# Value pages of a paged attention asked for two at a time behind pieces of the projections, and summed in twelve segments

## The chip, the core and the metric

The kernel runs on one core of a Trainium2 chip. Its time is the device time of one execution in microseconds (us). Before the change three runs took 2256.08, 2256.88 and 2257.73 us, a median of 2256.88. A profiled execution gives the order of the instructions on each engine: TensorE (PE for its matrix products, PEld for the loading of its stationary operand), VectorE (DVE), ScalarE (ACT), GpSimd (POOL), and SyncE (SP), whose queue asks for most transfers from HBM.

## The reference

The program is one step of a decoder layer for 256 prompt tokens and 8 sequences of 4 new tokens each, 288 columns in all, in float32:

```python
h = h + 1/2 * SwiGLU(RMSNorm(h))                     # half-step FFN 1
h = h + W_out[ norm(conv group) | norm(FoX group) ]  # token mixing
h = h + 1/2 * SwiGLU(RMSNorm(h))                     # half-step FFN 2
h = h + sigmoid(W_g RMSNorm(h)) * (W_p p[layer])     # per-layer input
```

The mixing projects the normed state to a short gated convolution (1024 columns each of B, C and h), to queries, keys and values of 8 heads of 128, and to forget gates. The prompt attends to itself. Each sample sequence attends to its new tokens and to 1024 past rows, which lie in 8 pages of 128 rows, picked by a page table:

```python
v_past = cache_v[page_table].reshape(DB, P, N_HEADS, HEAD_DIM)
...
p = jax.nn.softmax(s, axis=-1)
return jnp.einsum('bhqk,bkhd->bqhd', p.astype(v_all.dtype), v_all)
```

So 8 sequences of 8 pages, 64 value pages of 128 rows by 1024 floats (512 KB each), are multiplied by the probabilities and summed. The change is about how these 64 pages come in and when they are summed.

## The kernel before

**Products.** Every projection is computed with weights as the stationary operand and the 288 columns as the moving one. A weight piece is 512 KB: four blocks of 128 input features by 256 output features. SP loads it into a slot `raw0` to `raw6` (line 256), ACT and DVE split it into a high and a low part (line 294), and TensorE makes three products for each block and each half of the outputs (lines 340 and 342), 24 in all. The function `pair` makes the pieces for 256 outputs; one of its pieces is called a piece here. Splits run five half pieces ahead of the products.

**Order.** The program builds a list of steps. A step is a function, with the weights or pages that it needs. `run_steps` goes through the list, calls `load_upto` for as many items ahead as `state["ahead"]` says, and then the function. A planner afterwards orders the instructions of each engine by readiness, on its own estimate of times, and sets the semaphores; so the order of steps is a priority rather than a fixed order, except where a dependency is added by hand.

**The attention.** In the mixing the key, convolution, value and first half of the output projection form a list of 96 pieces, `fill`. Work of the attention is put between them with `at(i, ...)`, ahead of piece i. Key pages are read in eight pairs of sequences (line 761, up to piece 47). At 48 `v_start` opens the space for values. At 50 and 52 `probs_t` turns the probabilities, at 69 to 86 come the prompt heads.

**The values before.** `v_round` (line 818) sums one page of each of four sequences: round r of group gi takes page r of sequences 4 gi to 4 gi + 3. There are 16 rounds, at 51 and then every 2.7 pieces (round 12 at 82). A page has 1024 columns, two banks of 512. For each bank four products (line 828) with a stationary operand of 32 columns stand side by side in TensorE's four groups of 32 columns, one for each sequence, so a round is two fours. The trace records two instructions for each such product, 16 for a round. After the eighth round of a group `sample_out` adds the new tokens' values (line 841) and gathers the heads out of the two banks.

**The pages' way in.** A round's four pages are items in the same list as the weights. `load_upto` takes them in turn, and POOL asks for each with an indirect transfer (line 261). A page has one of seven slots: `raw4` to `raw6`, which the weights give up meanwhile (they rotate over four slots from the first page on), three of its own (`v0` to `v2`), and the place of the second group's scores, once these are turned. A request waits until the products of the slot's former page are done. POOL also does elementwise work of the convolution, of the residual and of the prompt's masks, all in one queue with the requests. `state["ahead"]` is 12 items, pages and weights together, from `v_start` on.

Of the kernel before, what the change touches and what calls it, by code (L numbers as in the profile page):

```python
# [16 lines left out]
F32 = mybir.dt.float32  # L17
# [8 lines left out]
P = 128  # L26
# [4 lines left out]
DT = 4  # L31
NS = DB * DT
# [4 lines left out]
PAGES = 8  # L37
# [6 lines left out]
RAW = 7  # L44
HALVES = 5
# [6 lines left out]
KPAIRS = (1, 8, 14, 21, 27, 34, 40, 47)  # L52
WEIGHTS = 4
VPAGES = 3
AHEAD = 12
WARM = (NT, NT, NT)
VSTEP = 2.7

GAINS = ("norm_mix", "norm_ffn2", "norm_ple", "norm_final", "norm_conv_out", "norm_attn_out", "conv_w")
A_ROWS = dict(norm_mix=D, norm_ffn2=D, norm_ple=D, norm_final=D, norm_conv_out=CB * P, norm_attn_out=NH * P,  # L60
# [36 lines left out]
def build(nc, tc, ctx, A, O):  # L97
# [3 lines left out]
    v, s, g, pe, sy = nc.vector, nc.scalar, nc.gpsimd, nc.tensor, nc.sync  # L101
# [43 lines left out]
    at = 0  # L145
# [92 lines left out]

    steps = []
    items = []  # L240
    state = dict(wslot=0, pages=0, through=False, ahead=RAW, loaded=0, split=0, used=0, halves_used=0, chunk=0, lead=HALVES)

    def load_upto(n, parts=None):
        while state["loaded"] < min(n, len(items)):
            it = items[state["loaded"]]
            if it["kind"] == "p" and "vx" not in W:
                return
            if it["kind"] == "w":
                state["wslot"] = (state["wslot"] + 1) % (WEIGHTS if state["pages"] and not state["through"] else RAW)
                t = rawp.tile([P, it["nk"], 256], F32, name="wraw", tag=f"raw{state['wslot']}")  # L250
                src = it["src"]
                if parts is not None:
                    cuts = (0, 1, 2, 3, 4) if state["loaded"] < 2 else (0, 2, 4)
                    parts.append([(t[:, a:b], src[:, a:b]) for a, b in zip(cuts, cuts[1:])])
                else:
                    d = sy.dma_start(t, src)
                    if state["used"] < 24:
                        tc.keep_in_program_order(d)
            else:
                t = page_tile()  # L260
                g.indirect_dma_start(out=t, out_offset=None, in_=it["src"],  # L261
                                     in_offset=bass.IndirectOffsetOnAxis(ap=it["rows"], axis=0))
            it["tile"] = t
            state["loaded"] += 1

    def page_tile():

# [42 lines left out]
    def page(src, j):  # L310
        return dict(kind="p", src=src, rows=idx[:, j:j + 1])

    def pair(src, c0, kts, act, evac, k_of=lambda k: k, late=0, tag="mm", rows_first=False):

        st = {}
        out = []
        chunks = [kts[i:i + 4] for i in range(0, len(kts), 4)]
        for ci, ks in enumerate(chunks):
            it = weight(src, ks[0], len(ks), c0)

            def fn(ci=ci, ks=ks, it=it, only=None):
                if ci == 0 and not only:
                    st["ps"] = [bank(tag, BANKS[tag]) for _ in range(2)]
                last = ci == len(chunks) - 1
                if only is None:
                    split_upto(state["halves_used"] + state["lead"])
                if not only:
                    state["chunk"] += 1
                for b in range(2):
                    o = st["ps"][b][:, :NT]  # L330
                    for j, k in enumerate(ks):
                        if only not in (None, j):
                            continue
                        hi, lo = it["parts"][j // 2 * 2]
                        w = slice(b * P, b * P + P)
                        xh, xl = act(k_of(k))
                        f = ci == 0 and j == 0
                        l = last and j == len(ks) - 1
                        for x in (xh, xl) if rows_first else (xl, xh):
                            pe.matmul(o, hi[:, j % 2, w], x, start=f, stop=False)  # L340
                            f = False
                        state["product"] = pe.matmul(o, lo[:, j % 2, w], xh, start=False, stop=l)  # L342
                    if only not in (None, len(ks) - 1):
                        continue
                    if b == 0:
                        run_deferred()
                    if last and late:
                        defer(lambda b=b, o=o: evac(b, o), late)
                    elif last:
                        evac(b, o)  # L350
                state["halves_used"] += len(ks) // 2 if only is None else only % 2

            if rows_first:
                out.extend(([] if j else [it], lambda j=j, fn=fn: fn(only=j)) for j in range(len(ks)))
                continue
            out.append(([it], fn))
        return out

# [457 lines left out]
                              t[:NS, :P].rearrange("s (c b x) -> s b c x", c=4, b=4)[:, b])  # L816
        M["PT", gi] = pt

    def v_round(gi, r):
        its = [page(A["cache_v"], (4 * gi + b) * PAGES + r) for b in range(4)]  # L820

        def fn():
            if r == 0:
                M["va", gi] = [bank("va", BANKS["va"]) for _ in range(2)]
                M["pv", gi] = M["PT", gi].rearrange("s (r b x) -> s r b x", b=4, x=32)
            for e in range(2):
                for b in range(4):
                    pe.matmul(M["va", gi][e][32 * b:32 * b + 32, :], M["pv", gi][:, r, b],  # L828
                              its[b]["tile"][:, e * 512:e * 512 + 512], start=r == 0, stop=False, tile_position=(0, 32 * b))
            if r == PAGES - 1:  # L830
                if gi == 1:
                    state.update(through=True, wslot=WEIGHTS - 1)
                sample_out(gi)
        return (its, fn)

    def sample_out(gi):
        mx = W["vv"][0]
        for b in range(4):
            for e in range(2):
                rows = slice(NS * e, NS * e + NS)  # L840
                pe.matmul(M["va", gi][e][32 * b:32 * b + 32, :], M["pv", gi][rows, 8, b], M["vs"][rows], start=False, stop=True,
                          tile_position=(NS * e, 32 * b))
        o = mx.tile([P, P], F32, name="so", tag="so", bufs=2)
        for hh in range(NH):
            src = M["va", gi][hh // 4][:, hh % 4 * P:hh % 4 * P + P]
            m = const("headmask")[:, hh:hh + 1]
            if hh == 0:
                v.tensor_scalar(o, src, m, None, ALU.mult)
            else:
                v.scalar_tensor_tensor(o, src, m, o, ALU.mult, ALU.add)  # L850
        defer(lambda: sample_turn(gi, o), 4 if gi == 0 else 2)

    def sample_turn(gi, o):
        mx = W["vv"][0]
        t = ktbank()
        pe.transpose(t[:, :P], o, ident)
        for half in range(2):
            v.tensor_copy(M["oS"][:, 4 * half:4 * half + 4, 16 * gi:16 * gi + 16].rearrange("p c (b t) -> p c b t", t=DT),
                          t[:, :P].rearrange("p (b c a t) -> p a c b t", c=4, a=2, t=DT)[:, half])
        if gi == 1:  # L860
            s.dma_start(O["v_prompt"].rearrange("(j p) c -> p j c", p=P), M["vn"])
            for e in range(2):
                s.dma_start(O["v_sample"][:, 512 * e:512 * e + 512], M["vs"][NS * e:NS * e + NS])
            for hh in range(NH):
                split(za[hh][0][:, SEQ:], za[hh][1][:, SEQ:], M["oS"][:, hh, :], gain("norm_attn_out", hh))
            sq = mx.tile([P, NH, NS], F32, name="sqS")
            s.activation(sq, M["oS"], AF.Square)
            v.tensor_reduce(acc[:, SEQ:], sq.rearrange("p h n -> p n h"), AX.X, ALU.add)
# [137 lines left out]
    def v_start():  # L1006
        for n in ("kq", "kt"):
            closed(n)
        opened("vv", "right")
        opened("vp", "right")  # L1010
        opened("vx", "right")
        state["ahead"] = AHEAD
        vv = W["vv"][0]
        M["vn"] = vv.tile([P, 2, NH * P], F32, name="vn")
        M["vs"] = vv.tile([2 * NS, NH * P // 2], F32, name="vs")
        M["oS"] = vv.tile([P, NH, NS], F32, name="oS")
# [25 lines left out]
    def at(i, *fns):  # L1042
        marks.setdefault(i, []).extend(fns)
# [37 lines left out]
    at(KPAIRS[3], lambda: new_scores(0), lambda: new_scores(1))  # L1081
    at(27, lambda: softmax(0))
    at(49, lambda: softmax(1))
    at(48, v_start)
    at(50, lambda: probs_t(0))
    at(52, lambda: probs_t(1))
    for r in range(2 * PAGES):
        at({12: 82}.get(r, int(51 + VSTEP * r)), v_round(r // PAGES, r % PAGES))
    for hh in range(NH):
        at(int(69 + 2.5 * hh), lambda hh=hh: prompt_head(hh))  # L1090
    at(80, lambda: norm_scale(rsc, acc2, CB * P, 2))
# [163 lines left out]
```

## Time and profile before

| What | us |
|---|---|
| Median of three runs | 2256.88 |
| The profiled execution | 2257.42 |
| Its span, first to last instruction | 2255.6 |
| TensorE busy with products | 2239.8 |
| Value products (line 828), 256 instructions, busy | 31.8 |
| Page requests on POOL (line 261), 64, busy | 64.6 |

Busy time of a group is the union of its instructions. Products are pipelined: each has a duration of some 290 ns while the next starts about 129 ns after it, so start-to-start distances tell what an instruction costs, not durations. A row of the order of time gives start, length, engine, line, operation, tiles, shape and count of instructions merged, and in brackets the engine's idle time before it with what ended it. A row of waits gives who waited for whom, the total in us, the number of times and the longest. A row on a stretch of time gives its length, each engine's busy time, TensorE's granted clock, the share of time in which the 16 transfer engines were busy, and GB/s.

### The profile page before, as it was taken

To read this page: it belongs to the slowest core of one execution; us is meant where nothing else is said; L and a number is where in the kernel's file an instruction comes from. 1 tells how busy PE (TensorE), PEld (TensorE's weight loads), DVE (VectorE), ACT (ScalarE), POOL (GpSimd) and SP (SyncE) were. 2 spreads that over 40 slices of the span, in tenths; PEclk is the share of its full clock that TensorE was granted. 3 is DMA by queue.
4 is the path that set the end of the run, shared out by engine and by line. 5 is a ranking of instruction groups with operands and counts; after the bars stand their busy time and mean duration, and the time that the engine had idled before them with its cause. 6 is when DMAs were issued, how large, how long until landed. Compare 5 with 4: busy or idle time off the path is not lost.

```text
span 2255.6 us, 44318 instructions
## 1 busy us (share of the span) xinstructions
PE 2239.8 (99%) x17387; PEld 2183.4 (97%) x17387; DVE 1343.2 (60%) x2413; ACT 1046.8 (46%) x1859; POOL 324.3 (14%) x399
## 2 busy tenths in 40 slices
PE   9999999999999999999999999999999999999997
PEld 9999999999999999888888999999999999999997
DVE  7555555555555686456566875555555555555865
ACT  6444444444444553344344554444444444444654
POOL 1020000000000113344446210000000000000211
PEclk9999999999999999999999999999999999999999
DMA  7575555555555546888988455545555555555552
GB/s 265 172 248 170 170 175 169 169 172 174 169 169 170 169 171 239 330 309 296 330 322 297 170 172 162 180 160 183 172 169 169 175 170 170 169 171 175 168 173 101
DMA packets 342850, 443.37 MB, mean 197 GB/s; under 512 B 17409, under 2 KB 307089, under 8 KB 342641
## 3 DMA queue, kind: packets, MB, share of 16 engines
q1 hardware_dynamic: 320928, 366.25, 49.3%
q0 software_dynamic: 20480, 71.67, 8.9%
q8 instruction: 136, 2.23, 0.4%
q10 hardware_dynamic: 1232, 2.62, 0.3%
q14 instruction: 74, 0.60, 0.1%
HBM read 435.41 MB, written 5.07 MB: 195 GB/s over the span
## 4 chain that ended last, share of the span: by engine, by line
PE 99%; DMA 1%; DVE 0%; issue 0%; ACT 0%; SPq 0%; DVEq 0%; ACTq 0%
PE mm L340 61%; PE mm L342 31%; PE va L340 1%; PE va L828 1%; PE va L761 1%; PE va L342 1%; DMA page<-in_cache_v_dram,idx 0%; PE kt L340 0%; DVE h L1181 0%; DMA h<-in_x_dram 0%; PE kt L342 0%; PE kt L882 0%; PE kt L915 0%; PE kt L906 0%; PE kt L881 0%
## 5 line engine op out<-in xcount | busy, mean ns | idle before, releaser
L340 PE MATMUL mm<-x,whi 128*128 128x288 f32 x7360 | 1430.5, 291 | 0.0
L294 DVE TENSOR_TENSOR wlo<-wraw,whi 128x512 fp32r<-128x512 f32 (+1 forms) x1388 | 975.9, 707 | 739.6 <-ACT whi L294 701.5
L294 ACT ACTIVATE whi<-wraw 128x512 fp32r<-128x512 f32 (+1 forms) x1388 | 861.8, 628 | 869.9 <-PE mm L340 782.6
L340 PEld LDWEIGHTS mm<-x,whi 128*128 128x128 f32 x7360 | 1163.4, 187 | 15.9 <-issue 13.5
L342 PE MATMUL mm<-x,wlo 128*128 128x288 f32 x3680 | 1067.4, 290 | 0.1
L342 PEld LDWEIGHTS mm<-x,wlo 128*128 128x128 f32 x3680 | 690.7, 188 | 0.3 <-DVE wlo L294 0.3
L340 PE MATMUL mm<-hid,whi 128*128 128x288 f32 x2816 | 544.8, 290 | 0.0
L340 PEld LDWEIGHTS mm<-hid,whi 128*128 128x128 f32 x2816 | 445.2, 187 | 0.0
L342 PE MATMUL mm<-hid,wlo 128*128 128x288 f32 x1408 | 408.3, 290 | 0.0
L412 POOL TENSOR_TENSOR sr<-sg,rs 128x288 f32<-128x288 f32 x88 | 71.6, 814 | 1383.7 <-ACT sg L410 1383.7
L342 PEld LDWEIGHTS mm<-hid,wlo 128*128 128x128 f32 x1408 | 264.3, 188 | 0.0
L432 DVE SCALAR_TENSOR_TENSOR h<-mm,h 128x288 f32<-128x288 f32 x192 | 85.6, 455 | 19.4 <-PE mm L342 19.4
L738 POOL DMA_INDIRECT KT<-in_cache_k_dram,idx x64 | 65.9, 1030 | 129.4 <-DVE idx L168 52.2
L410 ACT ACTIVATE sg<-tg 128x288 f32<-128x288 f32 x88 | 39.0, 444 | 97.9 <-DVE tg L408 97.8
L419 ACT ACTIVATE hid<-hd 128x288 fp32r<-128x288 f32 x88 | 39.2, 445 | 93.4 <-DVE hd L417 93.3
L234 POOL TENSOR_TENSOR acc<-acc,sq 128x288 f32<-128x288 f32 x52 | 44.0, 846 | 219.7 <-ACT sq L233 217.2
L261 POOL DMA_INDIRECT page<-in_cache_v_dram,idx x64 | 64.6, 1010 | 67.4 <-PE va L828 44.8
L420 DVE TENSOR_TENSOR hid<-hd,hid 128x288 fp32r<-128x288 f32 x88 | 40.2, 457 | 22.0 <-ACT hid L419 22.0
L340 PE MATMUL mm<-zc,whi 128*128 128x288 f32 x256 | 52.0, 297 | 0.0
L340 PE MATMUL va<-x,whi 128*128 128x288 f32 x256 | 51.1, 293 | 0.8 <-ACT whi L294 0.8
L417 DVE TENSOR_TENSOR hd<-mm,sr 128x288 f32<-128x288 f32 x86 | 39.1, 455 | 16.7 <-PE mm L342 16.7
L408 DVE TENSOR_TENSOR tg<-mm,rs 128x288 f32<-128x288 f32 x84 | 37.9, 452 | 14.1 <-PE mm L342 13.1
(237 smaller groups left out, 1061.0 us busy)
## 6 DMA issues: line engine op xcount, KB each, us to landing
wraw<-in_w_ffn_up_dram SPq DMA_DIRECT2D x173, 512.0 KB, 3.4
wraw<-in_w_ffn_gate_dram SPq DMA_DIRECT2D x172, 512.0 KB, 3.4
wraw<-in_w_ffn_down_dram SPq DMA_DIRECT2D x160, 512.0 KB, 3.2
wraw<-in_w_in_dram SPq DMA_DIRECT2D x96, 512.0 KB, 5.1
wraw<-in_w_out_dram SPq DMA_DIRECT2D x32, 512.0 KB, 4.5
wraw<-in_w_ple_gate_dram SPq DMA_DIRECT2D x32, 512.0 KB, 3.5
wraw<-in_w_ffn_down_dram SPq DMA_DIRECT2D x32, 256.0 KB, 2.7
wraw<-in_w_ple_proj_dram SPq DMA_DIRECT2D x8, 256.0 KB, 2.7
```

The lines of the kernel that those rows point to most:

```text
L234: (v if k >= KT - last_on_v else g).tensor_tensor(acc, acc, sq, ALU.add)
L261: g.indirect_dma_start(out=t, out_offset=None, in_=it["src"], in_offset=bass.IndirectOffsetOnAxis(ap=it["rows"], axis=0))
L294: for i in s.activation(hi, x, AF.Copy), v.tensor_tensor(lo, x, hi.bitcast(F32), ALU.subtract):
L340: pe.matmul(o, hi[:, j % 2, w], x, start=f, stop=False)
L342: state["product"] = pe.matmul(o, lo[:, j % 2, w], xh, start=False, stop=l)
L410: s.activation(u, t, AF.Silu)
L412: g.tensor_tensor(r, u, rs, ALU.mult)
L417: v.tensor_tensor(t, o, sg[b], ALU.mult)
L419: s.activation(H["hi"][:, k, :], t, AF.Copy)
L420: v.tensor_tensor(H["lo"][:, k, :], t, H["hi"][:, k, :].bitcast(F32), ALU.subtract)
L432: v.scalar_tensor_tensor(h[:, k, :], o, 0.5, h[:, k, :], ALU.mult, ALU.add)
L738: d = g.indirect_dma_start(out=t[:, i].rearrange("p h s -> p (h s)"), out_offset=None, in_=A["cache_k"], in_offset=bass.IndirectOffsetOnAx ...
```

## The change

- Pages leave the list of weights. `v_round` returns no items; its pages go to a list `wanted`. `load_upto` handles weights alone.
- A new `ask_pages` asks for pages in order, two at most, in each piece's function, after its splits and ahead of its products. The request is given a dependency on the last product made so far, that is, of the piece before. It asks only while fewer than six pages (seven from page 12 on) are asked and not yet taken up by a segment. At the head of a segment it is called once more for any page of the segment that is still missing, without that dependency.
- `v_round` takes any run of consecutive pages. `VENDS` cuts the 32 pages of each group into segments: 4, 4, 6, 6, 6, 6 in the first group and 6, 6, 6, 6, 4, 4 in the second. They are put at pieces 51, 53, 57, 61, 65, 69, 73, 78, 82, 86, 88 and 91.
- In the second bank the sequences are turned by two column groups, so that pages five and six of a segment fill four groups with their two halves. `sample_out` and `sample_turn` follow; the latter makes three copies in place of two for each group.
- The weights go over to four slots at piece 44 by an explicit switch, with 4 items ahead, and 6 items ahead (weights alone) from `v_start`, in place of 12 for both. Back to seven slots after the last segment, as before.

```diff
-AHEAD = 12
+VENDS = ((4, 8, 14, 20, 26, 32), (6, 12, 18, 24, 28, 32))
...
+    def ask_pages(count, upto=None):
+        while count and "vx" in W and state["pages"] < len(wanted):
+            n = state["pages"]
+            if n >= (state["eaten"] + (6 if n < 12 else 7) if upto is None else upto):
+                return
+            it = wanted[n]
+            it["tile"] = t = page_tile()
+            d = g.indirect_dma_start(out=t, out_offset=None, in_=it["src"],
+                                     in_offset=bass.IndirectOffsetOnAxis(ap=it["rows"], axis=0))
+            if upto is None:
+                tc.add_manual_dep(d.ins, state["product"].ins.name, mybir.DependencyInfo(
+                    mybir.DependencyClass.Sync, mybir.DependencyReason.DATA), reason="pace")
+            count -= 1
...
                 if only is None:
                     split_upto(state["halves_used"] + state["lead"])
+                    ask_pages(2)
...
-    def v_round(gi, r):
-        its = [page(A["cache_v"], (4 * gi + b) * PAGES + r) for b in range(4)]
+    def v_round(gi, pages):
+        its = [page(A["cache_v"], (4 * gi + n % 4) * PAGES + n // 4) for n in pages]
+        wanted.extend(its)
 
         def fn():
-            if r == 0:
+            ask_pages(len(wanted), state["eaten"] + len(pages))
+            state["eaten"] += len(pages)
+            if pages[0] == 0:
...
-            for e in range(2):
-                for b in range(4):
-                    pe.matmul(M["va", gi][e][32 * b:32 * b + 32, :], M["pv", gi][:, r, b],
-                              its[b]["tile"][:, e * 512:e * 512 + 512], start=r == 0, stop=False, tile_position=(0, 32 * b))
+            whole = [(i, e) for e in range(2) for i in (range(4) if e == 0 else (2, 3, 0, 1))]
+            for i, e in whole + [(i, e) for e in range(2) for i in range(4, len(pages))]:
+                r, b = divmod(pages[i], 4)
+                c = 32 * ((b + 2 * e) % 4)
+                pe.matmul(M["va", gi][e][c:c + 32, :], M["pv", gi][:, r, b], its[i]["tile"][:, e * 512:e * 512 + 512],
+                          start=r == 0, stop=False, tile_position=(0, c))
...
-        for half in range(2):
-            v.tensor_copy(M["oS"][:, 4 * half:4 * half + 4, 16 * gi:16 * gi + 16].rearrange("p c (b t) -> p c b t", t=DT),
-                          t[:, :P].rearrange("p (b c a t) -> p a c b t", c=4, a=2, t=DT)[:, half])
+        for half, to, at, n in (0, 0, 0, 4), (1, 0, 2, 2), (1, 2, 0, 2):
+            v.tensor_copy(M["oS"][:, 4 * half:4 * half + 4, 16 * gi:16 * gi + 16].rearrange("p c (b t) -> p c b t", t=DT)[:, :, to:to + n],
+                          t[:, :P].rearrange("p (b c a t) -> p a c b t", c=4, a=2, t=DT)[:, half][:, :, at:at + n])
...
-        state["ahead"] = AHEAD
+        state["ahead"] = WEIGHTS + 2
...
+    at(44, lambda: state.update(narrow=True, ahead=WEIGHTS))
...
-    for r in range(2 * PAGES):
-        at({12: 82}.get(r, int(51 + VSTEP * r)), v_round(r // PAGES, r % PAGES))
+    for gi, ends in enumerate(VENDS):
+        for a, b in zip((0,) + ends, ends):
+            at(int(51 + VSTEP * ((32 * gi + b) / 4 - 1)), v_round(gi, range(a, b)))
```

More of the change, by code (lines that the diff above doesn't have):

```diff
@@ L240, in build @@
     items = []
-    state = dict(wslot=0, pages=0, through=False, ahead=RAW, loaded=0, split=0, used=0, halves_used=0, chunk=0, lead=HALVES)
+    state = dict(wslot=0, pages=0, narrow=False, ahead=RAW, loaded=0, split=0, used=0, halves_used=0, chunk=0, lead=HALVES, eaten=0)
     def load_upto(n, parts=None):
@@ L245, in load_upto @@
             it = items[state["loaded"]]
[L246 to L258, printed above, removed]
-            else:
-                t = page_tile()
-                g.indirect_dma_start(out=t, out_offset=None, in_=it["src"],
-                                     in_offset=bass.IndirectOffsetOnAxis(ap=it["rows"], axis=0))
+            state["wslot"] = (state["wslot"] + 1) % (WEIGHTS if state["narrow"] else RAW)
@@ L263, in load_upto @@
+            t = rawp.tile([P, it["nk"], 256], F32, name="wraw", tag=f"raw{state['wslot']}")
+            src = it["src"]
+            if parts is not None:
+                cuts = (0, 1, 2, 3, 4) if state["loaded"] < 2 else (0, 2, 4)
+                parts.append([(t[:, a:b], src[:, a:b]) for a, b in zip(cuts, cuts[1:])])
+            else:
+                d = sy.dma_start(t, src)
+                if state["used"] < 24:
+                    tc.keep_in_program_order(d)
             it["tile"] = t
@@ L264, in load_upto @@
             state["loaded"] += 1
+    wanted = []
+    def ask_pages(count, upto=None):
[11 more added lines that the diff above has]
+            count -= 1
@@ L817, in probs_t @@
         M["PT", gi] = pt
-    def v_round(gi, r):
-        its = [page(A["cache_v"], (4 * gi + b) * PAGES + r) for b in range(4)]
+    def v_round(gi, pages):
+        its = [page(A["cache_v"], (4 * gi + n % 4) * PAGES + n // 4) for n in pages]
+        wanted.extend(its)
         def fn():
-            if r == 0:
+            ask_pages(len(wanted), state["eaten"] + len(pages))
+            state["eaten"] += len(pages)
+            if pages[0] == 0:
                 M["va", gi] = [bank("va", BANKS["va"]) for _ in range(2)]
                 M["pv", gi] = M["PT", gi].rearrange("s (r b x) -> s r b x", b=4, x=32)
-            for e in range(2):
-                for b in range(4):
-                    pe.matmul(M["va", gi][e][32 * b:32 * b + 32, :], M["pv", gi][:, r, b],
-                              its[b]["tile"][:, e * 512:e * 512 + 512], start=r == 0, stop=False, tile_position=(0, 32 * b))
-            if r == PAGES - 1:
+            whole = [(i, e) for e in range(2) for i in (range(4) if e == 0 else (2, 3, 0, 1))]
[4 more added lines that the diff above has]
+                          start=r == 0, stop=False, tile_position=(0, c))
+            if pages[-1] == 4 * PAGES - 1:
                 if gi == 1:
-                    state.update(through=True, wslot=WEIGHTS - 1)
+                    state.update(narrow=False, wslot=WEIGHTS - 1)
                 sample_out(gi)
-        return (its, fn)
+        return ([], fn)
     def sample_out(gi):
@@ L840, in sample_out @@
                 rows = slice(NS * e, NS * e + NS)
-                pe.matmul(M["va", gi][e][32 * b:32 * b + 32, :], M["pv", gi][rows, 8, b], M["vs"][rows], start=False, stop=True,
-                          tile_position=(NS * e, 32 * b))
+                c = 32 * ((b + 2 * e) % 4)
+                pe.matmul(M["va", gi][e][c:c + 32, :], M["pv", gi][rows, 8, b], M["vs"][rows], start=False, stop=True,
+                          tile_position=(NS * e, c))
         o = mx.tile([P, P], F32, name="so", tag="so", bufs=2)
```

## The prediction

> **What bounds the kernel now.** I read the page of the whole execution first, then the waits, then the order of time around the value pieces, because a change to one stage is worth only what that stage loses.
>
> ```profile
> span 2255.6 us, 44318 instructions
> ...
> PE 2239.8 (99%) x17387; PEld 2183.4 (97%) x17387; DVE 1343.2 (60%) x2413; ACT 1046.8 (46%) x1859; POOL 324.3 (14%) x399
> ...
> GB/s 265 172 248 170 170 175 169 169 172 174 169 169 170 169 171 239 330 309 296 330 322 297 170 172 162 180 160 183 172 169 169 175 170 170 169 171 175 168 173 101
> ...
> PE 99%; DMA 1%; DVE 0%; issue 0%; ACT 0%; SPq 0%; DVEq 0%; ACTq 0%
> ```
>
> TensorE is busy 99% of the span and is 99% of the chain that ended last. So only two things can move the time: the time TensorE spends on its own instructions, and the few places where it waits. Transfers run at about 170 GB/s outside the attention and at about 300 to 330 within it, which is where pages and weights share them. The next views are the waits: TensorE's from 800 to 1250 us, then all engines and SP's queue from 1040 to 1250 us.
>
> ```profile
> PE va L761 <- issue: 0.7, 1, 0.7
> PE va L828 <- DMA page<-in_cache_v_dram,idx: 0.6, 1, 0.6
> ```
> ```profile
> ACT whi L294 <- PE mm L340: 69.9, 42, 6.1
> ...
> POOL page L261 <- PE va L828: 44.8, 11, 7.0
> ```
> ```profile
> SPq L256 <- DVE wlo L294: 178.5, 44, 11.9
> ```
>
> TensorE waits once for a value page. ACT's splits of weights wait for TensorE and for no transfer of weights, and SP waits for slots to come free: weights are early. POOL stands 44.8 us in front of page requests whose slots the products of line 828 still hold. It is patience on an engine that nothing waits for long, so taking it away is worth nothing by itself.
>
> **Fewer pieces.** Before there are 16 rounds of four pages, after there are 4 segments of four and 8 of six. The 64 pages and their 256 recorded value instructions stay; what goes is four interruptions of the projection products. The order of time shows the price, with a pair of key sequences (32 instructions of the same shape) beside a value round (16).
>
> ```profile
> 1050.57 0.29 PE L342 MATMUL mm<-x,wlo 128*128 128x288 f32 x1
> ...
> 1050.95 0.29 PE L342 MATMUL mm<-x,wlo 128*128 128x288 f32 x1
> 1051.17 3.64 PE L761 MATMUL va<-KT,strip 128*32 128x512 f32 x32
> 1054.74 0.53 PE L340 MATMUL mm<-x,whi 128*128 128x288 f32 x2
> 1055.11 0.29 PE L342 MATMUL mm<-x,wlo 128*128 128x288 f32 x1
> ...
> 1068.10 0.29 PE L342 MATMUL mm<-x,wlo 128*128 128x288 f32 x1
> 1068.32 1.92 PE L828 MATMUL va<-page,PT 128*32 128x512 f32 x16
> 1070.17 0.54 PE L340 MATMUL mm<-x,whi 128*128 128x288 f32 x2
> 1070.55 0.30 PE L342 MATMUL mm<-x,wlo 128*128 128x288 f32 x1
> ```
>
> Three products take 0.38 us (1050.57 to 1050.95), 0.387 over longer stretches, so 0.129 each. From the last product before the round to the third after it 2.45 us pass (1068.10 to 1070.55), three of them worth 0.387: the round costs 2.06. The key pair costs 4.16 - 0.387 = 3.77. So 16 more instructions cost 1.71 us, and a round of 16 holds 2.06 - 1.71 = 0.35 us that belongs to entering and leaving. A six-page segment is 24 instructions: 0.35 + 1.5 x 1.71 = 2.92. Before: 16 x 2.06 = 33.0. After: 4 x 2.06 + 8 x 2.92 = 31.6. Gain **1.4 us**. This needs the groups of four columns to stay full. They do by the diff: the first four pages of a segment make two full fours, and pages five and six take two columns in each half, because the second half is turned by two columns. Were they not full, the odd pair would cost as two fours, 0.85 us more in each of eight segments, and the term would be a loss of 5.5; by the column arithmetic I rule that out. Upper bound 1.7, if an edge is worth 0.42.
>
> The turned columns cost DVE one more copy for each of the two groups.
>
> ```profile
> L858 DVE COPY oS<-kt x4: 215/218/225, 1161.8 to 1251.6; 128x64 f32<-128x64 f32 x4
> ```
> ```profile
> L340 PE MATMUL mm<-zal,whi x128: 293/293/293, 1262.3 to 1312.3; 128*128 128x288 f32 x128
> ```
>
> That is some 0.22 us. The last group's copies end at 1251.8 and their first reader among the products starts at 1262.3; about 10 us of products hide it, less the splits in between. Nothing.
>
> **The wait that goes.** One round is late.
>
> ```profile
> 1088.94 1.06 PE L828 MATMUL va<-page,PT 128*32 128x512 f32 x6
> 1090.62 1.90 PE L828 MATMUL va<-page,PT 128*32 128x512 f32 x10 [0.63 <-DMA page<-in_cache_v_dram,idx]
> 1092.46 0.53 PE L340 MATMUL mm<-x,whi 128*128 128x288 f32 x2
> ```
>
> It takes 3.52 us in place of the 1.85 of 1068.32 to 1070.17: 1.67 lost, of which the waits count 0.63 because the modelled tails of the first six cover the rest. Its page was asked for late, behind others:
>
> ```profile
> 1055.12 0.94 POOL L261 DMA_INDIRECT page<-in_cache_v_dram,idx  x1 [7.98 <-PE va L761]
> 1056.36 0.94 POOL L261 DMA_INDIRECT page<-in_cache_v_dram,idx  x1 [0.30 <-issue]
> ...
> 1070.51 1.04 POOL L261 DMA_INDIRECT page<-in_cache_v_dram,idx  x1 [5.03 <-PE va L828]
> ...
> 1082.34 0.94 POOL L261 DMA_INDIRECT page<-in_cache_v_dram,idx  x1 [0.30 <-PE mm L342]
> ```
> ```profile
> L261 POOL DMA_INDIRECT page<-in_cache_v_dram,idx x1: 941/941/941, 1082.3 to 1082.3; - x1
> ...
> DMA to landing us min/median/max: 8.2/8.2/8.2
> ```
>
> 1082.34 + 8.24 is 1090.6, the moment the round goes on. After, the segment that replaces it takes pages 8 to 13 at fill step 57, with 13 asked at step 54: three pieces (9.3 us) and the first two fours of the segment ahead of it. Gain **1.7 us**, bounds 0 and 1.7.
>
> **The new pacing.** Each request now waits for the last product of the piece before, two for a piece, with at most six or seven pages asked and not yet summed. Working the diff's counters through the fill steps: steps 48, 49, 50 ask for 0-1, 2-3, 4-5; each six-page segment sits four or five pieces behind the one before and its last page is the first of a pair asked two pieces ahead (page 19 at 59 for the segment at 61, 25 at 63, 31 at 67, 37 at 71, 49 at 80, 55 at 84; 43 at 75 has three). Two places are tighter: page 3 is the second of the pair at step 49, for the segment at 51 which reads it in its first four; page 59 is asked at step 87, **one** piece ahead of the segment at 88, again in the first four. What a page takes to land, over all 64, and for two single ones, the second of a burst at 1056.4 and the first of one at 1224.4:
>
> ```profile
> DMA to landing us min/median/max: 4.2/6.3/11.5
> ```
> ```profile
> L261 POOL DMA_INDIRECT page<-in_cache_v_dram,idx x1: 944/944/944, 1056.4 to 1056.4; - x1
> ...
> DMA to landing us min/median/max: 6.0/6.0/6.0
> ```
> ```profile
> L261 POOL DMA_INDIRECT page<-in_cache_v_dram,idx x1: 952/952/952, 1224.4 to 1224.4; - x1
> ...
> DMA to landing us min/median/max: 5.1/5.1/5.1
> ```
>
> And the last products that release the two tight requests, with the round that will want page 59:
>
> ```profile
> 1060.92 0.29 PE L342 MATMUL mm<-x,wlo 128*128 128x288 f32 x1
> ```
> ```profile
> 1227.03 0.29 PE L342 MATMUL mm<-zc,wlo 128*128 128x288 f32 x1
> ...
> 1231.02 1.92 PE L828 MATMUL va<-page,PT 128*32 128x512 f32 x16
> ```
>
> Page 3: released at 1061.21, POOL 0.3 later (as 1070.51 follows the round's end at 1070.24), one request of 1.25 ahead of it (1055.12 to 1056.36), so asked at 1062.75; with 6.0 it lands at 1068.75 and is wanted at 1068.4: **0.3 us** late. Bounds: 4.2 gives nothing, 8.2 gives 2.5. Page 59: released at 1227.32, asked at 1227.6, with 5.1 it lands at 1232.7, and the segment wants it at 1231.1: **1.6 us** late. Bounds: 4.2 gives 0.6, 8.2 gives 4.7; below that, nothing, if the planner puts the segment a little later. I take 5.1, measured at the same place in the fill. The ordinary six-page segment: two pieces are 2 x 24 x 0.129 = 6.2 us, the first two fours 1.7, less 0.6 for the release: a cover of 7.3 us against 4.2 to 6.0 for the first or second of a burst. No wait; at 8.2 it would be 0.9 each.
>
> The Trainium skill would put this lower. Its page "DMA: Bandwidth & Descriptors", section "Anatomy of one DMA — SWDGE (gpsimd) path", fits such a transfer as 2.0 us and its bytes at 436 GB/s, an estimate of 3.2 us for 512 KB; by it page 59 is on time and both lateness terms vanish. The trace's shortest page is 4.2 and its median 6.3, so the trace disagrees and decides.
>
> **What is queued behind the new waits.** They stand in POOL's one queue, so conv, residual and mask work behind a request waits until a piece has ended, at most 3.1 us. Today the same queue stands behind slots for up to 7.0 us at once, and no TensorE wait names POOL. Nothing. Weights keep four slots and a queue of their own; setting the narrow rotation at step 44 does not change which slot a weight gets, since weight 50 is the last one before the first page in either kernel. Bandwidth holds too:
>
> ```profile
> 1054.74:1246.26 191.52, 190.89 (x1481) 161.82 (x1477) 120.47 (x284) 77.82 (x161) 97.40 (x115) 1.00 0.85 304
> ```
> ```profile
> 1076.00:1086.00 10.00, 10.00 (x79) 8.40 (x79) 6.55 (x16) 4.70 (x10) 8.69 (x11) 1.00 0.95 356
> ```
>
> The stage moves 304 GB/s (last column) and has shown 356. A piece with two pages and a weight asks for 1.57 MB in some 3.1 us, above that, but only for two or three pieces of four or five.
>
> **The sum.** Own time of the profiled execution 2257.42 (span 2255.6 and 1.8 around it): - 1.4 - 1.7 + 0.3 + 1.6 = - 1.2, so 2256.2. That execution lies 0.54 above the median 2256.88, so the median comes to **2255.7**.
>
> **Rivals.** *All pages are early:* pairs land nearer 4.2 than today's bursts, or the planner puts the segment at 88 later. Then - 3.1: 2253.8. For it: requests come two at a time instead of four. Against it: 5.1 is itself a first of its burst. The skill's fit above ends here too.
>
> *Pages are late everywhere* (slower): the pairs go out while the weight queue is full and a page takes 8.2 us, as the one at 1082.34 did. Then six ordinary segments lose 0.9 each (5.4), page 3 loses 2.5 and page 59 4.7: 12.6 - 3.1 = + 9.5, 2266.4. It decides from 7.3 us of landing time on. For it: 1.57 MB per piece is over 356 GB/s, so a third pair finds a queue. Against it: the slow landings are those behind two or three other pages, and the wanted page is mostly the first of its pair.
>
> *The segments are not laid whole:* the planner orders TensorE by its own reckoning of arrivals; if it holds pages five and six or page 59 late, it breaks a segment with products between. A break costs 0.35, and 0.86 more where a four is torn: with five torn breaks 6.0 - 3.1 = + 2.9, 2259.8. Against it: all 16 rounds of before are whole, though their slots were given late.
>
> *It does not do what it says:* with the slots unchanged, requests still wait for slots, the late round stays late; only the 1.4 remains, 2255.5, beside the forecast.
>
> **Chances.** Forecast with the last rival 0.47 (2254.6 to 2257.5); all early 0.27; torn segments 0.13; late everywhere or something between 0.13 (from 2260 up). The range is **2253.0 to 2260.0**: below it lies only a gain that no row here shows, above it most of the late case. About 0.2% (4.5 us) is what a measurement of this kernel can tell from no change: faster by more than that 0.05, within it 0.83, slower 0.12.
>
> **What would show it.** Twelve value groups on TensorE, four of 1.85 us and eight near 2.71 from start to next start; no wait at the second or third; a wait of about 1.6 us at the eleventh and a trace of one at the first; POOL's page waits naming projection products instead of line 828's; a landing median below 6.3. Wrong would be: groups of other sizes, waits at the ordinary six-page segments, any TensorE wait on weights, or a change above 4.5 us.

## The result and the profile after

The changed kernel takes 2265.12 us (median of seven runs, 2262.92 to 2267.36). The kernel before takes 2256.89 beside it (2256.08 to 2257.84). The ratio is 1.0033, with an interval of 1.0024 to 1.0043: slower by some 8 us, where 2255.7 was forecast in a range up to 2260.0. The profiled executions are 2264.11 us after and 2257.42 before, 6.7 apart.

From the page of the changed kernel:

```profile
span 2262.3 us, 44304 instructions
...
PE 2243.3 (99%) x17387; PEld 2185.5 (97%) x17387; DVE 1342.5 (59%) x2415; ACT 1046.9 (46%) x1859; POOL 323.0 (14%) x399
...
PE 95%; issue 2%; DMA 1%; POOL 1%; DVE 1%; ACT 0%; POOLq 0%; DVEq 0%; ACTq 0%
```

TensorE is still busy 99% of the span, but it is 95% of the chain that ended last and no longer 99%: requests, transfers, POOL and VectorE have entered the chain. The waits from 1040 to 1270 us say where (line 843 is the value product, 268 the request for a page, 350 and 352 the products of the projections):

```profile
POOL page L268 <- PE va L843: 32.7, 8, 6.5
POOL page L268 <- PE mm L352: 23.6, 18, 4.2
...
PE va L843 <- DMA page<-in_cache_v_dram,idx: 3.4, 3, 1.8
...
PE mm L350 <- DVE zc L209: 0.5, 1, 0.5
PE kt L191 <- DVE sql L204: 0.4, 1, 0.4
```

POOL now waits for projection products (line 352) as the dependency asks, though still more for slots. TensorE waits for pages three times in place of once, and twice for VectorE, which it never did before in this stretch. The three late segments and a whole one, in order of time:

```profile
1069.18 1.92 PE L843 MATMUL va<-page,PT 128*32 128x512 f32 x6
1072.58 1.88 PE L843 MATMUL va<-page,PT 128*32 128x512 f32 x10 [1.48 <-DMA page<-in_cache_v_dram,idx]
1074.39 0.53 PE L350 MATMUL mm<-x,whi 128*128 128x288 f32 x2
...
1096.89 2.78 PE L843 MATMUL va<-page,PT 128*32 128x512 f32 x24
1099.61 0.53 PE L350 MATMUL mm<-x,whi 128*128 128x288 f32 x2
...
1128.85 2.76 PE L843 MATMUL va<-page,PT 128*32 128x512 f32 x18
1131.81 1.06 PE L843 MATMUL va<-page,PT 128*32 128x512 f32 x6 [0.19 <-DMA page<-in_cache_v_dram,idx]
1132.80 0.53 PE L350 MATMUL mm<-x,whi 128*128 128x288 f32 x2
...
1234.89 1.06 PE L843 MATMUL va<-page,PT 128*32 128x512 f32 x6
1237.72 1.90 PE L843 MATMUL va<-page,PT 128*32 128x512 f32 x10 [1.77 <-DMA page<-in_cache_v_dram,idx]
1239.56 0.54 PE L350 MATMUL mm<-zc,whi 128*128 128x288 f32 x2
```

A segment's cost is the distance from its first start to the start after it. The third is whole and takes 2.72 (1096.89 to 1099.61), as worked out: twelve segments stand there, none broken. The first takes 5.21 where 1.85 would do, the fifth 3.95 where 2.71 would do, the eleventh 4.67 where 1.85 would do. The three lose 3.36, 1.24 and 2.82, 7.4 us in all; the list of waits shows 3.4 of it, because the modelled tails of the first products cover the rest.

To compare stages without the noise of what lies ahead, the value stage is measured from the start of the last pair of key sequences to the start of the sums for the attention's norm (line 191). Before, the pair's row at 1051.17 is in the prediction, and the end is:

```profile
1257.38 0.29 PE L191 MATMUL kt<-sqh,meanr 128*128 128x288 f32 x1
```

After:

```profile
1052.03 3.64 PE L771 MATMUL va<-KT,strip 128*32 128x512 f32 x32
...
1264.09 0.29 PE L191 MATMUL kt<-sqh,meanr 128*128 128x288 f32 x1
```

That is 206.21 us before and 212.06 after, 5.85 more. The rest of the 6.7 lies ahead of the stage, whose last key pair starts 0.86 us later; what delays it was not followed up.

Why the first segment is late is seen in the transfers (share and GB/s are the last two columns):

```profile
1052.00:1056.00 4.00, 4.00 (x36) 1.33 (x36) 1.54 (x3) 0.63 (x1) 1.17 (x2) 1.00 0.49 156
1056.00:1060.00 4.00, 4.00 (x34) 4.00 (x33) 2.76 (x9) 1.59 (x3) 1.04 (x3) 1.00 0.24 53
1060.00:1064.00 4.00, 4.00 (x34) 4.00 (x33) 4.00 (x9) 2.25 (x4) 3.23 (x6) 1.00 0.60 187
1064.00:1068.00 4.00, 4.00 (x35) 3.99 (x34) 3.83 (x14) 1.88 (x4) 3.38 (x5) 1.00 0.91 323
1068.00:1072.00 4.00, 3.10 (x16) 1.30 (x14) 2.77 (x12) 1.26 (x2) 0.00 (x0) 1.00 1.03 417
```

From 1056 to 1060 us almost nothing moves, at 53 GB/s, where the kernel before moved 219 in the same stretch:

```profile
1056.00:1060.00 4.00, 4.00 (x33) 4.00 (x32) 2.92 (x11) 2.14 (x4) 3.37 (x7) 1.00 0.67 219
```

Then six pages and three weights are asked for within some seven us, and from 1068 on the transfers run full. The first request, and page 3's with its landing:

```profile
1059.75 1.15 POOL L268 DMA_INDIRECT page<-in_cache_v_dram,idx  x1 [1.24 <-ACT whi L303]
...
1063.88 1.08 POOL L268 DMA_INDIRECT page<-in_cache_v_dram,idx  x1 [0.30 <-issue]
```
```profile
L268 POOL DMA_INDIRECT page<-in_cache_v_dram,idx x1: 1077/1077/1077, 1063.9 to 1063.9; - x1
...
DMA to landing us min/median/max: 8.6/8.6/8.6
```

1063.88 and 8.57 make 1072.45, just ahead of 1072.58, when the segment goes on. In the kernel before three pages had already been asked for between 1042 and 1046 us, since their slots were free:

```profile
1042.42 1.25 POOL L261 DMA_INDIRECT page<-in_cache_v_dram,idx  x1 [0.16 <-issue]
...
1045.95 1.18 POOL L261 DMA_INDIRECT page<-in_cache_v_dram,idx  x1 [0.30 <-issue]
```

The new dependency and the condition on the value space put them at 1059.75 and later.

### The profile page after: what moved, and what is told of

Same layout as the page of the kernel before. It is cut to its first block, busy times and chain, and to the rows that moved or that the text cites. A ratio compares the mean times of both kernels' runs of the same rounds, so it can differ in the third digit from the quotient of the medians.

```text
span 2262.3 us, 44304 instructions
## 1 busy us (share of the span) xinstructions
PE 2243.3 (99%) x17387; PEld 2185.5 (97%) x17387; DVE 1342.5 (59%) x2415; ACT 1046.9 (46%) x1859; POOL 323.0 (14%) x399
## 4 chain that ended last, share of the span: by engine, by line
PE 95%; issue 2%; DMA 1%; POOL 1%; DVE 1%; ACT 0%; POOLq 0%; DVEq 0%; ACTq 0%
PE mm L350 59%; PE mm L352 30%; PE va L350 2%; PE va L771 1%; DMA page<-in_cache_v_dram,idx 1%; PE va L843 1%; POOL page L268 1%; PE va L352 1%; DMA KT<-in_cache_k_dram,idx 0%; PE kt L350 0%; DVE h L1199 0%; PE kt L352 0%; PE mm L530 0%; PE kt L898 0%; PE kt L931 0%
```

## The experiments

Three theories were set against each other, with a fourth added on the way. *Late pages*: TensorE loses by pages that are asked for too late. *Long segments*: runs of 24 value instructions cost by themselves. *Planner*: the order of VectorE and ScalarE around 1200 us changed, and that alone costs. *Lost cover*, added after the first five runs: with no value run at piece 80 any more, VectorE's work for the convolution's norm comes late. All kernels were timed in five rounds, four beside one another on one chip with the kernel before, whose median was 2257.14, 2258.02 and 2257.89 us in the three groups. So gains are told as distances to the kernel before of the same group; the change lies 8.2 us above its own. What a run of value products "loses" is read from the one profiled execution of each kernel, by distances between starts.

**Without the dependency.**

```diff
             d = g.indirect_dma_start(out=t, out_offset=None, in_=it["src"], ...)
-            if upto is None:
-                tc.add_manual_dep(d.ins, state["product"].ins.name, ..., reason="pace")
             count -= 1
```

> The changed kernel without the added dependency: a page is asked for as soon as its slot is free and the planner reaches it, still two for a piece in the order of steps; segments, slots and weights as in the change. Theory late pages (TensorE stands 7.4 us in front of pages asked too late, at the first, the fifth and the eleventh segment, against 1.7 before; the longer segments themselves save 1.4): the first segment's wait of 3.4 us goes and at least one of the other two shrinks, so 2258 to 2261 us from 2265.1. Theory long segments (a run of 24 value instructions starves the rest, whatever the supply): 2264 to 2266, with the twelve segments lengthened or the products after them late. Theory planner (the order of VectorE and ScalarE around 1200 us changed and costs 1.6 us): that lateness stays.

2259.81 us, ratio 1.0012 [1.0003, 1.0021], 2.7 us above the kernel before: some 5.5 us of the loss go with the dependency. The first segment waits for nothing; the second loses 1.1 and the eleventh 1.4; about 1.1 us of lateness at the norm stays.

**Paced, in sixteen runs of four.** `VENDS` is (4, 8, ..., 32) for both groups, and the runs stand where the rounds stood.

> The changed kernel with its pacing, but with sixteen runs of four pages at the pieces where the rounds stood before. Theory late pages: the first run is fed as in the change and keeps its wait of 3.4 us, the one at piece 88 now has its last page asked two pieces ahead in place of one and loses most of its 2.8, the fifth's 1.2 goes too; four more edges cost 1.4; together 2262 to 2264 us. Theory long segments: back at the kernel before, 2257.

2260.61 us, 1.0014 [1.0005, 1.0023]. That is below the range of late pages and 3.6 above the number of long segments, so neither was hit. Its value runs lose 3.8 us, 3.6 of them at the first run, where late pages expected 3.4; not expected was that the norm comes on time, which is worth about the distance to 2262. So the lateness at the norm goes with the twelve segments, and not with the pacing.

**Three pages early.** The condition on the value space is lifted for pages 0 to 2.

```diff
-        while count and "vx" in W and state["pages"] < len(wanted):
+        while count and ("vx" in W or state["narrow"] and state["pages"] < 3) and state["pages"] < len(wanted):
```

> The changed kernel, with pages 0 to 2 (whose slots are given up by the weights) asked for at pieces 45 and 46, two at a time and paced, before the value space is open; the rest as in the change. Theory late pages: between 1048 and 1060 us the transfers stood nearly empty (119, 156 and 53 GB/s), so three pages land there, the other three find the queue free, and the first segment's 3.4 us go: 2261 to 2262.5 us. Theory long segments: 2265.

2262.64 us, 1.0024 [1.0015, 1.0033], just above the range of late pages. The first segment takes 1.85 us, its 3.4 are gone. Page 3 is now asked for at

```profile
1058.34 1.03 POOL L268 DMA_INDIRECT page<-in_cache_v_dram,idx  x1 [0.72 <-PE mm L353]
```

which is 9.9 us ahead of its segment in place of 5.3, and it lands in 4.2 us in place of 8.6. This run shows the cause of the first segment's loss.

The eleventh lost 5.2 in this execution in place of 2.8, which hides part of the gain. Page 59 landed 0.9 us later behind its request than in the change, and behind the wait TensorE's granted clock (the third number from the end) was down:

```profile
1234.00:1238.00 4.00, 3.80 (x13) 0.98 (x14) 0.00 (x0) 0.00 (x0) 0.95 (x1) 0.59 1.01 408
```

It stood at half for 3.4 us, an estimate of some 1.5 us lost. Over the whole execution this is a mean clock of 0.997, which eight of this kernel's eleven runs have, and none of the 33 of the kernel before beside it.

**The eleventh segment at 89.** `at(89, ...)` for pages 56 to 59 in place of 88.

> The changed kernel with the eleventh segment (pages 56 to 59) one piece later, at 89, so that page 59 is asked two pieces ahead of it in place of one. Theory late pages: its 2.8 us of waiting go, nothing else changes: 2262 to 2263 us. Theory long segments: 2265.

2263.09 us, 1.0026 [1.0017, 1.0035], a little above the range of late pages. The eleventh loses 0.7 in place of 2.8, and the twelfth, now nearer behind it, 0.6.

**Both repairs.**

> Both repairs at once, pacing kept: pages 0 to 2 asked at pieces 45 and 46, and the eleventh segment at 89. Theory late pages with additive waits: the two repairs alone took 2.5 and 2.0 us off 2265.1, together 2259.5 to 2261 us; value waits left below 2.5 us. If the gains are not additive, because a segment that is early makes the next one late: 2262 or more.

2258.35 us, 1.0002 [0.9993, 1.0011]. With both, the loss against the kernel before is no longer to be seen, with pacing and segments as in the change. The value runs lose 3.15 us in the profiled execution, where below 2.5 was expected; the median is below the expected range all the same. Against the kernel before, the gain on the change is 7.9 us, more than the single gains of 2.7 and 2.3 together. Part of the difference is the eleventh segment, which with the three early pages alone lost more than in the change.

**Both repairs without the dependency, then with the ninth segment at 81, and in sixteen runs.** These three were to bring the twelve segments under the kernel before.

> As the kernel with both repairs, and without the added dependency. Theory late pages: the value waits left without the dependency (1.1 at the second and 1.4 us at the eleventh segment) go too, 2257 to 2258.5 us from 2259.8. Theory lost cover (no value run stands at piece 80 any more, so VectorE's work for the convolution's norm comes 1.4 us late for TensorE at about 1200 us): that lateness stays, so the kernel doesn't get under the one before by more than 0.5 us though it has four runs fewer.

> As the kernel before it in this list, with the ninth segment at piece 81 in place of 82, ahead of the products that need the last convolution block and of the norm's sums. Theory lost cover: the 1.4 us at about 1200 us go, 2255.5 to 2257 us. If that lateness came from VectorE's order alone and not from missing products in front of it: no change.

> As the sixth kernel (no added dependency, three pages early), with sixteen runs of four at the pieces of the rounds before. Theory of edges: four more runs cost 1.4 us against twelve segments without the lateness of the norm, and nothing against twelve with it, so 2256.5 to 2258.5 us, within 1 us of the sixth kernel and 1.4 above the seventh. Theory long segments: 2 us or more under the sixth.

2261.75 us, 1.0018 [1.0009, 1.0028]; 2265.08 us, 1.0028 [1.0018, 1.0038]; 2261.45 us, 1.0016 [1.0007, 1.0025]. All three missed upward. In each the second run loses 2.6 to 3.0 us. In the first of them the page that it waits for is the one asked for at 1073.52, ahead of POOL's convolution work, and ahead of it in turn stands a request (1070.89) for a page of the third run:

```profile
1070.89 1.04 POOL L268 DMA_INDIRECT page<-in_cache_v_dram,idx  x1 [4.44 <-PE va L841]
...
1073.52 0.95 POOL L268 DMA_INDIRECT page<-in_cache_v_dram,idx  x1 [0.30 <-issue]
1074.49 0.75 POOL L983 TENSOR_TENSOR tB<-tB,cy 128x256 f32<-128x256 f32 x1
```
```profile
1080.97 1.90 PE L841 MATMUL va<-page,PT 128*32 128x512 f32 x10 [1.60 <-DMA page<-in_cache_v_dram,idx]
```

So without the dependency the planner asks for pages out of their order, and the awaited page is in 7.45 us after its request (7.0 to 7.5 in the three). The kernel without the dependency and without early pages has the same order; there it took 5.5 us, and the run lost 1.05. Why it takes longer here is not shown. With the dependency the requests follow the order of pages.

Around the norm the first of them has 4.7 us left over beyond its value runs and the second 7.4, the third nothing (the table below). The waits of the one with the ninth segment at 81:

```profile
PE mm L348 <- DVE tB L1065: 3.5, 1, 3.5
PE va L841 <- DMA page<-in_cache_v_dram,idx: 1.5, 1, 1.5
```

A value run at 81 is ahead of the sums, and the sums come at 1208.07 and 1208.28, close together. But the norm's result was later than ever: TensorE waits 3.5 us for an evacuation (line 1065) that needs it. In VectorE's queue the norm's last steps (lines 197 to 199) stand behind a split of weights that itself waits for TensorE:

```profile
1213.42 0.69 DVE L301 TENSOR_TENSOR wlo<-wraw,whi 128x512 fp32r<-128x512 f32 x1 [3.33 <-PE kt L930]
```

Behind TensorE's wait the granted clock was at half, for 6.8 us:

```profile
1216.00:1222.00 6.00, 5.51 (x23) 5.50 (x24) 3.20 (x6) 1.53 (x3) 4.09 (x7) 0.50 0.58 213
```

Products start 0.24 us apart there in place of 0.129, an estimate of some 2.6 us lost. With 3.65 for the wait, by starts, and 1.0 in short waits ahead of the norm this is nearly all of the 7.4. The first of the three has waits of 1.8 and 0.55 us at the norm, 3.4 us at half clock behind them (some 1.6 lost), and 0.5 ahead. So missing products alone don't explain the lateness; the planner's order of VectorE has a part in it, and the clock adds to it.

**Three pages behind a piece.** `ask_pages(3)`, all else as in the change.

> The changed kernel with three pages asked behind a piece in place of two, all else as in the change. Page 59 is then asked two pieces ahead of its segment, page 3 as the first of the second three. Theory late pages, set by how early a page is asked: the eleventh segment's 2.8 us go, the first's 3.4 stays between 2 and 3.4 because its pages and the weights behind them still start from an empty queue at piece 48; 2261 to 2263 us. If the bunching of requests is what delays a page, three at a time land later: 2266 or more.

2261.85 us, 1.0017 [1.0008, 1.0026], as late pages expected: the first segment still loses 3.1, the eleventh 0.9 in place of 2.8. Asking for three at a time did no harm here; what counts is how early a page is asked for.

**Segments of four at 80 and 82.** Three behind a piece, pages 0 to 2 early, and

```diff
-VENDS = ((4, 8, 14, 20, 26, 32), (6, 12, 18, 24, 28, 32))
+VENDS = ((4, 8, 14, 20, 26, 32), (6, 12, 16, 20, 26, 32))
```

> Pacing kept at three for a piece, pages 0 to 2 early, and the second group's four-page segments moved to pieces 80 and 82 (segments at 73, 78, 80, 82, 87, 91, still twelve in all), so that a value run stands at 80 as in the kernel before. Theory lost cover: the lateness of 1.4 us at about 1200 us goes, with value waits below 2.5: 2256 to 2257.5 us. Theory that the lateness is the planner's order and comes with any twelve segments: 2258 to 2259.

2260.68 us, 1.0015 [1.0005, 1.0024]: above the ranges of both theories, but the lateness at the norm is gone, with twelve segments. Order of time around it, with the value run of the kernel before at 80, the changed kernel, and this one:

```profile
1194.79 1.92 PE L828 MATMUL va<-page,PT 128*32 128x512 f32 x16
...
1202.32 0.38 PE L191 MATMUL kt<-sqh,meanr 128*128 128x288 f32 x1
1202.53 0.29 PE L191 MATMUL kt<-sql,meanr 128*128 128x288 f32 x1
```
```profile
1202.94 0.53 PE L350 MATMUL mm<-zc,whi 128*128 128x288 f32 x2 [0.47 <-DVE zc L209]
...
1203.78 0.40 PE L191 MATMUL kt<-sqh,meanr 128*128 128x288 f32 x1
1204.54 0.40 PE L191 MATMUL kt<-sql,meanr 128*128 128x288 f32 x1 [0.35 <-DVE sql L204]
```
```profile
1201.19 0.38 PE L191 MATMUL kt<-sqh,meanr 128*128 128x288 f32 x1
1201.40 0.30 PE L191 MATMUL kt<-sql,meanr 128*128 128x288 f32 x1
```

The second sum starts 0.21 us after the first before and in this kernel, 0.76 after in the changed one, and there the products ahead of it wait too. What the stage holds more is the value runs, which lose 3.6 us in the profiled execution. That execution, at 2258.35 us, is the quickest of the eleven; what the others hold more no trace shows.

**Paced rounds with three pages early, and the mixed form.** Sixteen runs of four, paced at two; then segments in the first group and eight runs of four in the second, fourteen runs.

> Sixteen runs of four as before the change, paced at two, with pages 0 to 2 early: the paced rounds without their one wait of 3.6 us. Theory late pages: 2256.5 to 2258 us, no different from the kernel before by more than 1 us, perhaps below it by the 1.7 of its one late round. If the pacing costs something beside its late pages: 2259 or more.

> Paced at two, pages 0 to 2 early, segments of four and six in the first group and eight rounds of four in the second: fourteen runs, with value runs at 80 and 82 and no page asked one piece ahead. Theory of edges with lost cover: 0.7 us below the sixteen paced rounds with early pages, 2255.5 to 2257.5. If six-page segments cost by themselves: 1 us or more above them.

2256.95 us, 0.9996 [0.9987, 1.0005], and 2257.47 us, 1.0001 [0.9992, 1.0010]. Neither can be told from the kernel before. The second lies 0.5 above the first, between the two theories (0.7 below, or 1 or more above): in the profiled execution its runs lose 1.5 us more, against 0.7 that two runs fewer save. The first has no value wait left; its stage and its landings:

```profile
1053.52 3.64 PE L772 MATMUL va<-KT,strip 128*32 128x512 f32 x32
```
```profile
1258.07 0.29 PE L191 MATMUL kt<-sqh,meanr 128*128 128x288 f32 x1
```
```profile
DMA to landing us min/median/max: 4.3/6.9/10.4
```

204.55 us, 1.66 under the kernel before, just what its one late round cost (1.67). So pacing costs nothing by itself. It even helps once the first pages are early: the same sixteen runs without the dependency lie 3.4 us above the kernel before, these 0.9 below. Its pages land no sooner, at a median of 6.9 us against 6.3 (of the 56 of 64 landings that the trace holds); they are only asked for early enough.

**The sum closes.** Sixteen runs without a value wait are 206.21 - 1.73 = 204.48 us of stage. Without the losses of their value runs, the kernels with 14 and 12 runs and a value run at piece 80 come to 203.75 and 203.11 us. So each run fewer saves about 0.34; the table takes 0.335, and the prediction's 0.35 would close within 0.1 us as well. With the losses of value runs read as above, the rest is left over:

| Kernel | Runs | Stage, us | Value runs lose | Left over |
|---|---|---|---|---|
| before | 16 | 206.21 | 1.73 | (0) |
| the change | 12 | 212.06 | 7.43 | 1.5 |
| without the dependency | 12 | 206.65 | 2.46 | 1.1 |
| paced rounds | 16 | 208.24 | 3.78 | 0.0 |
| three early | 12 | 210.96 | 6.36 | 1.5 |
| eleventh at 89 | 12 | 210.39 | 5.81 | 1.4 |
| both repairs | 12 | 207.78 | 3.15 | 1.5 |
| both, no dependency | 12 | 211.24 | 3.37 | 4.7 |
| the same, ninth at 81 | 12 | 214.21 | 3.68 | 7.4 |
| early rounds, no dependency | 16 | 207.63 | 3.15 | 0.0 |
| three behind a piece | 12 | 208.79 | 4.80 | 0.9 |
| fours at 80 and 82 | 12 | 206.73 | 3.62 | 0.0 |
| paced rounds, early | 16 | 204.55 | 0.07 | 0.0 |
| six, then rounds | 14 | 205.28 | 1.53 | -0.1 |

What is left over lies around the norm. Of the 4.7 and 7.4 us some 1.6 and 2.6 are the half clock, and 0.5 and 1.0 are short waits ahead of the norm; the loss of the kernel with three early holds some 1.5 of half clock too. In the changed kernel starts from 1202 to 1205 us show 1.2 of its 1.5, and no such fall of the clock.

All six kernels with a value run at piece 80 have nothing left over, whether they hold 12, 14 or 16 runs; all eight without one have 0.9 us or more. Long segments as a cause of their own have no room: the kernel with fours at 80 and 82 closes at 0.0 with eight six-page segments. Whether the run at 80 helps by its 1.85 us of products or by the order of VectorE that the planner makes with it, no run separates; the kernel with the ninth segment at 81 shows that a late place in VectorE's queue alone cost a wait of 3.5 us, with some 2.6 us of half clock behind it.

## Why the prediction was wrong

The direction and the range were wrong; by the prediction's own steps:

- **Fewer pieces, - 1.4.** Right. Segments took 1.85 and 2.71 where nothing was late, none was torn, the fours stayed full, and the table closes with 0.335 for each run less.
- **The wait that goes, - 1.7.** Right: the third segment, which replaces that round, waits for nothing.
- **Page 3, + 0.3.** The step that failed most: 3.4 us. The mechanism and the time of the request were right: 1062.75 was worked out, and with the key pairs 0.9 later it was 1063.88. The landing was mis-sized, 8.6 us for 6.0. The 6.0 came from a row at 1056 of before, when three of the six pages were already in; with all six asked for behind an empty stretch the transfers filled to 417 GB/s. That the change moves pages 0 to 2 by some 16 us was in the counters of the text, and what this does to the landings was not worked out. The upper bound of 2.5 was too low as well. The run with three pages early shows that this is the cause: page 3 landed in 4.2 us and the loss was gone.
- **Page 59, + 1.6.** Mechanism and place right, size off: 2.8, as the page took 6.2 us and not 5.1.
- **The ordinary six-page segment, "no wait".** Wrong once in the profiled execution: 1.24 us at the fifth, whose last page took 9.4 us against a cover of 7.3.
- **What was not in the sum:** the norm's lateness, 1.5 us. The text counted what a segment costs TensorE and not what the round at 80 hid for VectorE. It cancels the whole gain from fewer segments. With a value run at piece 80 again, it was gone.
- **Queues, weights and copies, nothing.** Right for weights: no TensorE wait names one in the stage. The most that transfers had shown was not 356 GB/s, though: the kernel before moved 416 from 1150 to 1160 us. The turned copies have 5.6 us of cover and not 10, since by the kernel the sums at 1257.38 need them too; they still cost nothing. For POOL the paced kernel without late pages shows that the new waits cost nothing.
- **The rivals.** Late pages everywhere (2266.4) came nearest, with a chance of 0.13 and the right deciding point, but waits stood at three segments rather than eight. That the landing median would fall below 6.3 was wrong: it stayed at 6.3.
- **The skill's fit.** The estimate of 3.2 us for a page from the Trainium skill, "DMA: Bandwidth & Descriptors", section "Anatomy of one DMA — SWDGE (gpsimd) path", was further from the trace than the row chosen: the quickest page after took 4.4 us and the slowest 10.3. The fit has no term for what else is on the way.

In the profiled executions the sum is now - 1.4 - 1.7 + 7.4 + 1.5 = + 5.8 for the stage, against 5.85 measured, and 0.9 ahead of it. It closes in part by its making, since the 1.5 is what the other terms leave over. The medians lie 8.2 apart; the changed kernel's runs spread over 4.4 us where those of before spread over 1.8, which fits waits that hang on landing times, but no run shows it for a single execution. Short falls of the clock may be part of it: the mean granted clock of its two slowest runs is 0.997 and of the other five 0.998. No such run of it was traced.

## What to carry to other kernels

When a change delays requests, a landing time from the old trace is not a price for the new one: it was measured with part of the traffic already done, so the price has to be worked out with all that is then asked for together. What an early request buys is mainly lead: the paced rounds lost their whole wait by asking for three pages earlier, while the median landing stayed no quicker. Only the pages that then found the transfers nearly empty also landed sooner, as page 3 did. And work that is moved on the bounding engine leaves a hole for the engines that it hid; look at what becomes due in the next piece before counting the move as a gain. A wait can cost more than its length, if the clock falls behind it, so read the granted clock there before giving the loss one cause.

## What the runs showed of the hardware

- The transfers carried 417 GB/s over 4 us with weights and pages mixed, at a share of 1.03 of the sixteen engines' time. Between 1059.75 and 1066.99 us six pages were asked for in a row, and landing grew from 5.2 to 10.3 us from first to last.
- An excursion from projection products to value products of 32 columns costs 0.335 us in entering and leaving. With it the stages of all kernels whose norm is on time close to within 0.1 us, at 12, 14 and 16 runs.
- A wait of TensorE in the profile can be less than half of what it costs: 1.48 us are shown for the first segment's loss of 3.36.
- TensorE's granted clock fell to half behind some waits of the stage: for 3.4 us behind one of 2.3 us (three pages early), for 6.8 behind one of 3.5 (ninth segment at 81), and for 3.4 behind one of 1.6 with a second of 0.35 after it (both repairs without the dependency). Behind the single waits of up to 1.8 us in the other kernels' stages it stayed at full. By the distances between starts such a fall costs some 1.5 to 2.6 us more, an estimate.
